# Encoder trunk of two layers: a second plain FFN set, the output projection's first half by weight chunks, and an earlier load of the first norm's scale and shift

## The chip, the cores and the metric

One core of a Trainium2 chip runs the whole kernel in one launch. Times are device microseconds (us). TensorE (PE in the profile) multiplies matrices, VectorE (DVE) and ScalarE (ACT) do elementwise work, GpSimd (POOL) small work, and SyncE (SP) issues all DMA transfers here. Each engine takes its own instructions in the order in which they stand in its queue; engines wait for each other by semaphores.

## The reference, cut to what matters

```python
x = layer_norm(x, ln_in_g, ln_in_b)                 # x: 512 tokens x 1024
for l in range(2):
    proj = x @ w_in[l]                              # 6816 columns: q, k, v of three mixers, and gates
    ...                                             # neighbourhood, differential and latent attention
    merged = sum(gates[b] * (out[b] @ w_branch[l, b]) for b in range(3))
    x = layer_norm(ALPHA * x + merged @ w_out[l], ln1_g[l], ln1_b[l])
    gu = x @ w_ffn_in[l]                            # 2 x 2816 columns
    hidden = silu(gu[..., :2816]) * gu[..., 2816:]
    x = layer_norm(ALPHA * x + hidden @ w_ffn_out[l], ln2_g[l], ln2_b[l])
```

All in float32.

## The kernel before, in words

**Products.** Each float32 operand is held as two parts, hi and lo, and a product of two matrices is three matmuls (hi by hi, hi by lo, lo by hi; `mm3`, lines L156 to L158, or `product`, L778). ACT writes hi (a copy, L138 or L221) and DVE writes lo (a difference, L139 or L222). A matmul works on 128 rows of the contraction and on up to 512 columns. The tokens are four tiles t of 128; the transposed x stands in `xth` and `xtl` as eight contraction tiles k.

**Buffers.** A weight chunk of 128 x 1024 is loaded by SP into one of two `raw` buffers, and split into one of four `whi` and one of four `wlo` buffers (`wload`, `wsplit`), or, with `wload_slots`, into slots of the pool R (38 tiles of 128 x 512), where it can stay longer. The pool H has eight tiles of 128 x 1024 (`f` in the profile; `r` is a slot of R). PSUM has four kinds of banks, two of each: `acc`, `sc`, `pv` and `tr`. A matmul that begins a new sum in a bank waits until the last sum has been read from it.

**Order.** The program is written in the order of the functions. A scheduler of the framework then places each engine's instructions, by readiness in its own model of time and by priority (`high_priority`, used in `wsplit` unless `now` is false), so an engine's queue mixes what the text has apart.

**The output projection** (`out_proj`, L701). After the merges (`merge`; L685 and L686 on DVE take the merge sums out of `acc`, ACT L224 and DVE L225 split the merged tiles into R), x times ALPHA plus the product with `w_out` is formed in two halves of 512 columns. A half's weights are four chunks of two contraction tiles. For each token tile, one `acc` bank takes 8 x 3 matmuls through all four chunks, and DVE (L711) adds it to x. Between the halves `ahead` loads the first FFN set's weights into R (`plain_weights`, four `raw` loads, each split by two ACT and two DVE instructions). After each tile of the second half, `layer_norm` (L237 statistics, L239, POOL, L252, L253) and `to_xt` (L263 transposes into `tr`, then L221 and L222 into `xth` and `xtl`) follow.

**The FFN** goes by sets of 256 gate and 256 up columns, eleven per layer. The first set is plain (`ffn_plain`): gate and up by direct products, for two halves of the tokens, in the banks `sc` and `pv`. The other ten use seven products for eight (`ffn_fast`, after Strassen), for which sums and differences of weight quarters (L839 to L841, L853) and of x's quarters (`x_sums`, four sums, each of eight R slots, from `gt` and `xs` tiles; L748 to L759 on DVE) are formed and split. In the second set, the first to use the sums, `early` is true: the products that use no sum come first, the gate's second quarter among them, and `x_sums` is called in the middle of the set. Sets go in chunks of 3, 3, 3 and 2; a chunk's product with `w_ffn_out` (`ffn_down`) stands among the next chunk's sets.

**The start.** SP issues the first x tile (L278), the tables `cons` (L282, 256 KB: the identity that the transposes use, and rotary tables), then scale and shift of the first norm (`load_gb`, L270, twice 512 KB), the second x tile, and the first weights. For tile 0, DVE's L252 needs the scale and L253 the shift; the transposes L263 need `cons` and L253's result.

Of the kernel before, what the change touches and what calls it, by code (L numbers as in the profile page):

```python
# [12 lines left out]
OP = mybir.AluOpType  # L13
# [8 lines left out]
NT = 4  # L22
KD = 8
# [58 lines left out]
def trunk(ctx, tc, x, ln_in, w_in, feat, bias, lamv, w_mla, w_mlr, w_mlv, w_branch, w_out,  # L82
# [37 lines left out]
        return dp.tile([128, 512], F32, tag="P", name="P", bufs=4)  # L120


    def wload(segs, nk, ncol):
        raw = wp.tile([128, 1024], F32, tag="raw", name="raw", bufs=2)
        rv = raw[:, :nk * ncol].rearrange("p (k c) -> p k c", k=nk)
        c = 0
        for src in segs:
            w = src.shape[1]
            nc.sync.dma_start(rv[:, :, c:c + w], src.rearrange("(k p) c -> p k c", p=128))
            c += w  # L130
        hi, lo = wsplit(raw, nk * ncol)
        return hi.rearrange("p (k c) -> p k c", k=nk), lo.rearrange("p (k c) -> p k c", k=nk)

    def wsplit(raw, n, now=True):
# [9 lines left out]
        nc.sync.dma_start(raw[:, :n], src)  # L144
        return wsplit(raw, n)

    def wload_ks(src_of, widths, steps):

        res, k = [], 0
        for n in steps:  # L150
            res.append((k, n, wload(src_of(k * 128, (k + n) * 128), n, widths)))
            k += n
        return res

# [124 lines left out]

    G.memset(expo, -0.5)  # L280
    load_x(0)
    nc.sync.dma_start(cons, cst)  # L282
    gb = load_gb(ln_in)
    na_v, na_slots = [], []
    load_x(1)
    na_v += na_value_chunks(0, (0,))
# [414 lines left out]
    def out_proj(xt, mg, l, ahead):  # L701
        act = tuple(KTiles(m) for m in mg)
        for hf in range(2):
            if hf == 1:
                ahead()
            c = slice(hf * 512, (hf + 1) * 512)
            ch = wload_ks(lambda a, e: [w_out[l, a:e, c]], 512, (2, 2, 2, 2))
            for t in range(NT):
                p = bank("acc")
                gemm_x(p, ch, slice(0, 512), act, tsl(t), KD)  # L710
                V.scalar_tensor_tensor(xt[t][:, c], xt[t][:, c], ALPHA, p, op0=OP.mult, op1=OP.add)  # L711
                if hf == 1:
                    yield t
        R.put(*mg[0], *mg[1])


# [70 lines left out]
        split(*hl, sg)  # L787
        return hl

    def plain_weights(l, m):  # L790

        chs, slots = [], []
        for base in (0, D_FF):
            c = slice(base + m * 128, base + (m + 2) * 128)
            ch, sl = wload_slots(lambda a, e: [w_ffn_in[l, a:e, c]], 256, (4, 4))
            chs.append(ch)
            slots += sl
        return chs, slots

    def ffn_plain(chs, slots):  # L800
# [12 lines left out]
    def ffn_fast(l, m, sums):  # L813


        early = not sums

        def load(t, base, kh):
            c = slice(base + m * 128, base + (m + 2) * 128)
            nc.sync.dma_start(t.rearrange("p (k c) -> p k c", k=4),  # L820
                              w_ffn_in[l, kh * 512:(kh + 1) * 512, c].rearrange("(k p) c -> p k c", p=128))
            return t

        def halved(t, now=True):
            return wsplit(t, 1024, now)

        g0, u0, u1 = load(H.get(), 0, 0), load(H.get(), D_FF, 0), load(H.get(), D_FF, 1)
        s = H.get()
        g1 = load(wp.tile([128, 1024], F32, tag="raw", name="raw", bufs=2), 0, 1)
        px, py, pz = bank("sc"), bank("pv"), bank("sc")  # L830
        product(px, halved(g0, not early), from_x(0, 0), True)
        p1 = ptile()
        A.activation(p1, px, AF.Copy)  # L833
        if early:
            product(px, halved(g1, False), from_x(1, 0), False)
            sums += x_sums()
        t1, t2, t3, t4 = sums
        with tc.high_priority():
            V.tensor_add(s, u0, u1)  # L839
            V.tensor_sub(u0, g0, u0)  # L840
            V.tensor_sub(g0, s, g0)  # L841
        product(py, halved(g0), from_sum(t2), True)
        u2 = ptile()
        V.tensor_add(u2, py, p1)  # L844
        product(pz, halved(s), from_sum(t1), True)
        product(py, halved(u0), from_sum(t3), False)
        u3 = ptile()
        V.tensor_add(u3, py, p1)
        V.tensor_add(u3, pz, u3)
        if not early:  # L850
            product(px, halved(g1), from_x(1, 0), False)
        with tc.high_priority():
            V.tensor_sub(g1, g1, g0)  # L853
        product(pz, halved(g1), from_x(1, 1), False)
        V.tensor_add(u2, pz, u2)
        product(py, halved(u1), from_sum(t4), False)
        V.tensor_add(p1, py, p1)
        H.put(s, u0, g0, u1)
        res = [hidden(px, p1)]
        res.append(hidden(u2, u3))  # L860
        return res
# [24 lines left out]
    for l in range(DEPTH):  # L886
# [21 lines left out]
        mg = [[], []]  # L908
# [57 lines left out]
            nc.sync.dma_start(xt[t], xd[t])  # L966
        gb = load_gb(ln1[l])
        plain = []
        for t in out_proj(xt, mg, l, lambda: plain.append(plain_weights(l, 0))):
            layer_norm(xt[t], *gb)  # L970
            to_xt(xt[t], t)
        H.put(*gb)
        done, sums = None, []
        for c, (m0, n) in enumerate(CHUNKS):
            sets = []
            for i in range(n):
                m = 2 * (m0 + i)
                if m0 + i == 0:
                    sets.append(ffn_plain(*plain[0]))
                else:  # L980
                    sets.append(ffn_fast(l, m, sums))
                last = m0 + i == D_FF // 256 - 1
# [107 lines left out]
```

## Time and profile before

| what | value |
|---|---|
| three timed runs | 1859.96 us median (1859.23 to 1865.12) |
| the profiled execution's own time | 1861.61 us |
| its span, first to last instruction | 1859.6 us |
| mean granted TensorE clock | 0.996 |
| PE, DVE, ACT, POOL busy | 98%, 72%, 49%, 5% of the span |
| matmuls | 11200 |

The profile lists each engine's instructions with start and duration in us from the span's start. A line of the waits says who waited for whom, how long in total, how often, and the longest. A row of a group or of the timeline names the source line, the engine, the operation, the tile written and the tiles read, and the shapes; in brackets stands how long the engine was idle before it and who ended that. Matmuls are pipelined: one begins before the record of the last one has ended. The granted clock is the share of full speed that TensorE's clock had in a stretch. The chain is the work that ended last, followed back from the end, each piece with its start and duration.

### The profile page before, as it was taken

How to read it: one execution, taken by the hardware profiler on the slowest of the kernel's cores; microseconds unless marked ns; L12 is line 12 of the kernel's file. 1: busy time of each engine (PE TensorE's matmuls, PEld its weight loads, DVE VectorE, ACT ScalarE, POOL GpSimd, SP SyncE). 2: the span in 40 equal slices, each digit the busy share in tenths (PEclk: the TensorE clock that was granted, in tenths of full speed). 3: DMA queues.
4: the chain of work that ended last, by engine and by line, in shares of the span. 5: the costliest groups of instructions: out<-in, count | busy, mean ns of one | idle time of the engine just before them, and what ended most of it. 6: DMA issues, size and time to landing. Idle time of an engine off the chain costs nothing.

```text
span 1859.6 us, 28547 instructions
## 1 busy us (share of the span) xinstructions
PE 1814.6 (98%) x11200; PEld 1617.4 (87%) x11200; DVE 1331.0 (72%) x2228; ACT 905.3 (49%) x1620; POOL 88.2 (5%) x165
## 2 busy tenths in 40 slices
PE   6999999999999899999999999999999999999997
PEld 5988899988878899999789888999888789999996
DVE  6478887665568977777756888866655698677766
ACT  3467776555433433434326677755554244343431
POOL 4100000000001000000001000000000000000001
PEclk9999999999999999999999999999999999999999
DMA  7453332223251233333445432322233512333332
GB/s 250 119 166 88 88 101 74 79 81 85 90 193 58 69 104 101 102 103 102 148 124 156 124 97 87 90 65 86 74 97 109 174 57 90 105 95 110 92 101 79
DMA packets 167765, 195.86 MB, mean 105 GB/s; under 512 B 8528, under 2 KB 132688, under 8 KB 167632
## 3 DMA queue, kind: packets, MB, share of 16 engines
q1 hardware_dynamic: 167632, 194.05, 34.5%
q8 instruction: 88, 1.44, 0.3%
q14 instruction: 45, 0.37, 0.1%
HBM read 177.24 MB, written 9.44 MB: 100 GB/s over the span
## 4 chain that ended last, share of the span: by engine, by line
PE 89%; DVE 4%; DMA 3%; ACT 2%; issue 1%; POOL 1%; POOLq 0%; SPq 0%; DVEq 0%; ACTq 0%
PE acc L156 18%; PE acc L157 18%; PE acc L158 18%; PE sc L778 11%; PE pv L778 8%; PE tr L648 2%; DVE wlo L139 1%; PE pv L491 1%; DMA raw<-in_w_ffn_in_dram 1%; ACT whi L138 1%; PE pv L656 1%; PE pv L655 1%; PE sc L477 1%; PE sc L632 1%; PE sc L631 1%
## 5 line engine op out<-in xcount | busy, mean ns | idle before, releaser
L139 DVE TENSOR_TENSOR wlo<-raw,whi 128x1024 fp32r<-128x1024 f32 (+4 forms) x242 | 288.0, 1191 | 137.0 <-ACT whi L138 132.2
L138 ACT ACTIVATE whi<-raw 128x1024 fp32r<-128x1024 f32 (+4 forms) x242 | 250.0, 1034 | 267.4 <-DMA raw<-in_w_ffn_out_dram 50.9
L138 ACT ACTIVATE whi<-f 128x1024 fp32r<-128x1024 f32 x100 | 104.9, 1057 | 222.4 <-PE acc L158 127.3
L156 PE MATMUL acc<-xth,whi 128*128 128x512 f32 x512 | 203.9, 398 | 0.1
L158 PE MATMUL acc<-xth,wlo 128*128 128x512 f32 x512 | 202.8, 396 | 0.0
L157 PE MATMUL acc<-xtl,whi 128*128 128x512 f32 x512 | 202.6, 396 | 0.0
L156 PE MATMUL acc<-whi,r 128*128 128x512 f32 (+1 forms) x504 | 194.7, 392 | 4.6 <-DVE f L711 3.9
L157 PE MATMUL acc<-wlo,r 128*128 128x512 f32 (+1 forms) x504 | 197.3, 391 | 1.1 <-DVE wlo L139 1.1
L158 PE MATMUL acc<-whi,r 128*128 128x512 f32 (+1 forms) x504 | 197.0, 391 | 0.0
L778 PE MATMUL pv<-r,whi 128*128 128x256 f32 x960 | 175.8, 282 | 9.9 <-DVE P L844 4.8
L156 PE MATMUL acc<-whi,xth 128*128 128x256 f32 (+2 forms) x544 | 161.6, 299 | 2.1 <-ACT whi L138 2.1
L157 PE MATMUL acc<-wlo,xth 128*128 128x256 f32 (+2 forms) x544 | 162.1, 299 | 1.3 <-DVE wlo L139 1.3
L158 PE MATMUL acc<-whi,xtl 128*128 128x256 f32 (+2 forms) x544 | 162.1, 299 | 0.0
L778 PEld LDWEIGHTS pv<-r,whi 128*128 128x128 f32 x960 | 148.2, 189 | 13.4 <-DVE P L844 5.2
L139 DVE TENSOR_TENSOR wlo<-f,whi 128x1024 fp32r<-128x1024 f32 x100 | 121.6, 1221 | 26.0 <-ACT whi L138 25.8
L778 PE MATMUL pv<-r,wlo 128*128 128x256 f32 x480 | 134.7, 281 | 0.0
L778 PE MATMUL sc<-xth,whi 128*128 128x256 f32 x480 | 133.9, 280 | 0.7 <-ACT P L833 0.7
L778 PE MATMUL sc<-xtl,whi 128*128 128x256 f32 x480 | 133.7, 279 | 0.0
L778 PE MATMUL sc<-xth,wlo 128*128 128x256 f32 x480 | 133.3, 279 | 0.0
L156 PEld LDWEIGHTS acc<-whi,r 128*128 128x128 f32 x504 | 94.3, 188 | 26.9 <-DVE f L711 4.7
L157 PEld LDWEIGHTS acc<-wlo,r 128*128 128x128 f32 x504 | 95.0, 188 | 22.1 <-DVE wlo L139 1.8
L158 PEld LDWEIGHTS acc<-whi,r 128*128 128x128 f32 x504 | 94.9, 188 | 21.0
(235 smaller groups left out, 4285.3 us busy)
## 6 DMA issues: line engine op xcount, KB each, us to landing
raw<-in_w_in_dram SPq DMA_DIRECT2D x64, 512.0 KB, 3.8
f<-in_w_ffn_in_dram SPq DMA_DIRECT2D x60, 512.0 KB, 3.7
raw<-in_w_ffn_out_dram SPq DMA_DIRECT2D x44, 512.0 KB, 3.8
raw<-in_w_in_dram SPq DMA_DIRECT2D x64, 256.0 KB, 3.3
raw<-in_w_ffn_in_dram SPq DMA_DIRECT2D x28, 512.0 KB, 3.6
raw<-in_w_branch_dram SPq DMA_DIRECT2D x24, 512.0 KB, 3.5
raw<-in_w_out_dram SPq DMA_DIRECT2D x16, 512.0 KB, 3.8
r<-r SPq DMA_DIRECT2D x56, 128.0 KB, 2.9
```

The lines of the kernel that those rows point to most:

```text
L138: A.activation(hi[:, :n], raw[:, :n], AF.Copy)
L139: V.tensor_sub(lo[:, :n], raw[:, :n], f32(hi[:, :n]))
L156: T.matmul(o, lh[0], rh[0], start=first, stop=False)
L157: T.matmul(o, lh[0], rh[1], start=False, stop=False)
L158: T.matmul(o, lh[1], rh[0], start=False, stop=last)
L477: T.matmul(sc, qs[j][:, tsl(t)], ks[j][1], start=False, stop=True)
L491: T.matmul(po[:, 0:256], ch_[:, tsl(k)], v, start=k == 0, stop=False)
L631: T.matmul(sc, q[0][:, tsl(t)], k[0], start=True, stop=False)
L632: T.matmul(sc, q[0][:, tsl(t)], k[1], start=False, stop=False)
L648: T.transpose(pt[:, tsl(i)], prs[i % 2][:, tsl(kp + i // 2)], ident)
L655: T.matmul(oc, v, ph[:, c], start=kt == 0, stop=False)
L778: T.matmul(o[:, c], w[a][:, j, f], x[e], start=fresh and mi == 0 and j == 0 and n == 0, stop=j == 3 and n == 2, skip_group_check=True)
```

## The change

Three things. (1) The second FFN set is computed plainly too: its weights are streamed through the `raw`, `whi` and `wlo` buffers without high priority, and `x_sums` is called once, after that set, so `ffn_fast` loses its `early` form. (2) In the first half of the output projection the loop over weight chunks is the outer one and the four token tiles are summed side by side in two `sc` and two `pv` banks; `ahead` is called within the first half, behind its loads. The second half is as before. (3) Scale and shift of the first norm are issued ahead of the tables.

```diff
@@ wload, wload_ks
-    def wload(segs, nk, ncol):
+    def wload(segs, nk, ncol, now=True):
...
-        hi, lo = wsplit(raw, nk * ncol)
+        hi, lo = wsplit(raw, nk * ncol, now)
@@ start
     load_x(0)
+    gb = load_gb(ln_in)
     nc.sync.dma_start(cons, cst)
-    gb = load_gb(ln_in)
@@ out_proj
         for hf in range(2):
-            if hf == 1:
-                ahead()
             c = slice(hf * 512, (hf + 1) * 512)
             ch = wload_ks(lambda a, e: [w_out[l, a:e, c]], 512, (2, 2, 2, 2))
+            if hf == 0:
+                ahead()
+                ps4 = [bank(i) for i in ("sc", "sc", "pv", "pv")]
+                for part in ch:
+                    for t in range(NT):
+                        gemm_x(ps4[t], [part], slice(0, 512), act, tsl(t), KD)
+                for t in range(NT):
+                    V.scalar_tensor_tensor(xt[t][:, c], xt[t][:, c], ALPHA, ps4[t], op0=OP.mult, op1=OP.add)
+                continue
             for t in range(NT):
                 p = bank("acc")
                 gemm_x(p, ch, slice(0, 512), act, tsl(t), KD)
                 V.scalar_tensor_tensor(xt[t][:, c], xt[t][:, c], ALPHA, p, op0=OP.mult, op1=OP.add)
-                if hf == 1:
-                    yield t
+                yield t
@@ plain_weights
-    def plain_weights(l, m):
+    def plain_weights(l, m, ahead):
...
-            ch, sl = wload_slots(lambda a, e: [w_ffn_in[l, a:e, c]], 256, (4, 4))
+            src = lambda a, e: [w_ffn_in[l, a:e, c]]
+            if ahead:
+                ch, sl = wload_slots(src, 256, (4, 4))
+                slots += sl
+            else:
+                ch = wload_ks(src, 256, (4, 4), False)
             chs.append(ch)
-            slots += sl
@@ ffn_fast
-        early = not sums
...
-        product(px, halved(g0, not early), from_x(0, 0), True)
+        product(px, halved(g0), from_x(0, 0), True)
...
-        if early:
-            product(px, halved(g1, False), from_x(1, 0), False)
-            sums += x_sums()
...
-        if not early:
-            product(px, halved(g1), from_x(1, 0), False)
+        product(px, halved(g1), from_x(1, 0), False)
@@ the layer's loop
                 if m0 + i == 0:
                     sets.append(ffn_plain(*plain[0]))
+                elif m0 + i == 1:
+                    sets.append(ffn_plain(*plain_weights(l, m, False)))
+                    sums = x_sums()
                 else:
                     sets.append(ffn_fast(l, m, sums))
```

What it moves in the queues, at the places that the prediction speaks of. First PE, at the end of layer 0's merges (a space: the row stands in both; +: only in the changed program). The `acc` rows are merges, the `sc` and `pv` rows the projection's first half, which read the merged tiles `r`.

```order
 L157 MATMUL acc<-r_85,whi 128x512
 L158 MATMUL acc<-r_84,wlo 128x512
+L157 MATMUL sc<-wlo,r_94 128x512
+L158 MATMUL sc<-whi,r_95 128x512
+L156 MATMUL pv<-whi,r_94 128x512
+L157 MATMUL pv<-wlo,r_94 128x512
+L158 MATMUL pv<-whi,r_95 128x512
+L158 MATMUL pv<-whi,r_87 128x512
+L156 MATMUL pv<-whi,r_94 128x512
 L156 MATMUL acc<-r_108,whi 128x512
```

These are seven of the 26 first-half matmuls that now stand between merges, and so ahead of the last merge's end; 24 + 46 follow it. Next DVE, a little later: the sums of the first half in the old program, between the splits of the first FFN set's weights (`r<-raw`).

```order
 L222 TENSOR_TENSOR r_111<-raw,r_110 128x512
 L222 TENSOR_TENSOR r_93<-raw,r_92 128x512
-L711 SCALAR_TENSOR_TENSOR f_115<-f_115,acc 128x512
-L711 SCALAR_TENSOR_TENSOR f_117<-f_117,acc 128x512
-L237 BN_STATS ring<-f_115 128x6
-L237 BN_STATS ring<-f_117 128x6
 L222 TENSOR_TENSOR r_107<-raw,r_106 128x512
 L222 TENSOR_TENSOR r_109<-raw,r_108 128x512
```

The first-half sums (L711, now L713) stood behind three of the four splits and are now behind all four, among the splits of the second half's weights (`wlo<-raw`):

```order
+L139 TENSOR_TENSOR wlo<-raw,whi 128x1024
+L713 SCALAR_TENSOR_TENSOR f_115<-f_115,sc 128x512
+L139 TENSOR_TENSOR wlo<-raw,whi 128x1024
+L237 BN_STATS ring<-f_115 128x6
+L713 SCALAR_TENSOR_TENSOR f_117<-f_117,sc 128x512
+L713 SCALAR_TENSOR_TENSOR f_118<-f_118,pv 128x512
+L237 BN_STATS ring<-f_117 128x6
+L713 SCALAR_TENSOR_TENSOR f_116<-f_116,pv 128x512
 L237 BN_STATS ring<-f_118 128x6
-L139 TENSOR_TENSOR wlo<-raw,whi 128x1024 x2
-L711 SCALAR_TENSOR_TENSOR f_116<-f_116,acc 128x512
+L139 TENSOR_TENSOR wlo<-raw,whi 128x1024
```

Six rows of L713 and L237 now stand between the second half's second and third `wlo`. Last DVE again, where the norm of the last two token tiles meets the second set's weights.

```order
 L253 SCALAR_TENSOR_TENSOR f_118<-f_118,ring,f_114 128x512
 L222 TENSOR_TENSOR xtl<-tr,xth 128x4x128
 L253 SCALAR_TENSOR_TENSOR f_118<-f_118,ring,f_114 128x512
+L139 TENSOR_TENSOR wlo<-raw,whi 128x1024
 L237 BN_STATS ring<-f_116 128x6
+L139 TENSOR_TENSOR wlo<-raw,whi 128x1024
+L222 TENSOR_TENSOR xtl<-tr,xth 128x4x128 x2
```

Two splits of the second plain set's weights stand ahead of the next copies of `xtl`, and so of the last tile's norm.

More of the change, by code (lines that the diff above doesn't have):

```diff
@@ L145, in wload_flat, with wload_ks @@
         return wsplit(raw, n)
-    def wload_ks(src_of, widths, steps):
+    def wload_ks(src_of, widths, steps, now=True):
         res, k = [], 0
         for n in steps:
-            res.append((k, n, wload(src_of(k * 128, (k + n) * 128), n, widths)))
+            res.append((k, n, wload(src_of(k * 128, (k + n) * 128), n, widths, now)))
             k += n
@@ L822, in load, with halved @@
             return t
-        def halved(t, now=True):
-            return wsplit(t, 1024, now)
+        def halved(t):
+            return wsplit(t, 1024)
         g0, u0, u1 = load(H.get(), 0, 0), load(H.get(), D_FF, 0), load(H.get(), D_FF, 1)
@@ L968, in trunk @@
         plain = []
-        for t in out_proj(xt, mg, l, lambda: plain.append(plain_weights(l, 0))):
+        for t in out_proj(xt, mg, l, lambda: plain.append(plain_weights(l, 0, True))):
             layer_norm(xt[t], *gb)
@@ L972, in trunk @@
         H.put(*gb)
-        done, sums = None, []
+        done = None
         for c, (m0, n) in enumerate(CHUNKS):
```

## The prediction

> **What bounds the kernel now.** I read the page first: busy time, and the chain that ended last.
>
> ```profile
> span 1859.6 us, 28547 instructions
> PE 1814.6 (98%) x11200; PEld 1617.4 (87%) x11200; DVE 1331.0 (72%) x2228; ACT 905.3 (49%) x1620; POOL 88.2 (5%) x165
> PE 89%; DVE 4%; DMA 3%; ACT 2%; issue 1%; POOL 1%; POOLq 0%; SPq 0%; DVEq 0%; ACTq 0%
> ```
>
> TensorE is busy for all but 45.0 us. So a change can gain only where PE waits, where its clock is down, or by fewer matmuls; this one adds matmuls. The stretches (us, PE busy, PEld, DVE, ACT, POOL, granted clock, DMA share, GB/s) show where PE waits near the edits: layer 0's output projection, then layer 0's second FFN set, then the same two places of layer 1.
>
> ```profile
> 535.00:540.00 5.00, 4.27 (x19) 3.08 (x17) 1.72 (x3) 2.25 (x4) 0.00 (x0) 1.00 1.07 349
> 540.00:545.00 5.00, 3.48 (x9) 2.76 (x10) 4.45 (x8) 1.21 (x3) 0.00 (x0) 0.70 0.39 127
> 545.00:550.00 5.00, 5.00 (x22) 4.01 (x22) 1.00 (x2) 0.00 (x0) 0.00 (x0) 0.96 0.33 105
> ...
> 605.00:610.00 5.00, 4.78 (x43) 4.58 (x41) 5.00 (x9) 3.29 (x6) 0.00 (x0) 1.00 0.00 0
> ...
> 615.00:620.00 5.00, 2.57 (x20) 2.16 (x18) 5.00 (x8) 3.27 (x4) 0.00 (x0) 1.00 0.34 105
> 620.00:625.00 5.00, 3.09 (x24) 2.89 (x24) 4.97 (x6) 0.12 (x1) 0.00 (x0) 1.00 0.02 3
> 625.00:630.00 5.00, 4.58 (x38) 4.58 (x39) 3.53 (x6) 2.49 (x3) 0.00 (x0) 1.00 0.00 0
> ```
> ```profile
> 1455.00:1460.00 5.00, 3.39 (x16) 2.40 (x15) 3.22 (x6) 2.10 (x4) 0.00 (x0) 1.00 0.85 268
> ...
> 1525.00:1530.00 5.00, 4.50 (x38) 4.31 (x37) 4.39 (x7) 2.39 (x5) 0.00 (x0) 1.00 0.36 110
> 1530.00:1535.00 5.00, 3.52 (x28) 3.11 (x26) 4.92 (x7) 3.02 (x6) 0.00 (x0) 1.00 0.37 105
> 1535.00:1540.00 5.00, 2.76 (x18) 2.76 (x19) 4.97 (x6) 0.82 (x1) 0.00 (x0) 0.87 0.01 2
> 1540.00:1545.00 5.00, 4.22 (x30) 3.92 (x30) 3.23 (x4) 1.54 (x2) 0.00 (x0) 0.79 0.00 0
> ```
>
> PE misses 2.25 us in the projection of layer 0 and 1.61 in layer 1; at the second set it misses 4.98 (605 to 630) and 4.98 (1525 to 1545). There DVE is full: PE waits for it. The clock column counts too: 0.70 and 0.96 of 5 us are 1.7 us of lost cycles after layer 0's projection wait, 0.87 and 0.79 another 1.7 us in layer 1's second set.
>
> **The change part by part.** The price of a matmul is its interval in a run without a wait, from the chain (start, us, what) and from two successive starts:
>
> ```profile
> 628.51 5.65 PE sc L778 x48
> ```
> ```profile
> 577.18 0.39 PE L157 MATMUL acc<-wlo,r 128*128 128x512 f32 x1
> 577.41 0.39 PE L158 MATMUL acc<-whi,r 128*128 128x512 f32 x1
> ```
>
> So 0.118 us for 256 columns, 0.23 for 512. A record lasts 0.16 us longer than its interval, so each wait costs 0.16 more than the idle time shown.
>
> *More matmuls.* A set by seven products is 7 x 2 x 4 x 3 = 168 matmuls of 256 columns, a plain one 2 x 2 x 2 x 8 x 3 = 192. The 24 more cost half of that 5.65 us row: 2.83 per layer, **+5.65** in all, on PE, with nothing to hide them.
>
> *The second set's waits.* They are waits for DVE, which makes the sums of x while PE already needs them. After the change the sums are made under a plain set that reads none of them, 192 x 0.118 = 22.6 us. The first and the last row of that DVE work:
>
> ```profile
> 592.20 0.68 DVE L748 TENSOR_TENSOR gt<-xth 128x512 f32<-128x512 f32 x1
> ...
> 618.82 0.68 DVE L222 TENSOR_TENSOR r<-gt,r 128x512 fp32r<-128x512 f32 x1
> ```
>
> It took 27.3 us, with splits for the set itself in between, which no longer press. All waits go: 4.98 + 4.98, four waits per layer at 0.16 (1.3), and the clock's 1.7: **-13.0**. What is late next there is nothing I can find: the third set's first buffer for weights comes free when the plain set's gate half ends, 48 matmuls (5.65) before it starts, and a split needs 2.3.
>
> *The projection.* Who ended its waits:
>
> ```profile
> PE acc L156 <- DVE f L711: 2.2, 1, 2.2
> ```
>
> The sums L711 that free the two banks stand in DVE's queue behind splits that wait for weights. With four banks in the first half and acc in the second, that wait goes, in both layers: 2.25 + 1.61 + 0.3 + 1.7 of clock = **-5.9**. But the loads themselves don't get faster, and I ask who is late next. The rows, all of layer 0 but the last two:
>
> ```profile
> 522.43 1.07 ACT whi L138
> 523.52 1.24 DVE wlo L139
> 524.78 4.69 DMA raw<-in_w_ffn_in_dram
> ...
> 533.21 5.67 DMA raw<-in_w_ffn_in_dram
> ...
> 1442.62 4.77 DMA raw<-in_w_ffn_in_dram
> ...
> 1451.13 4.96 DMA raw<-in_w_ffn_in_dram
> ```
> ```profile
> 528.10 0.69 DVE L685 SCALAR_TENSOR_TENSOR f<-f,acc 128x512 f32<-128x512 f32 x1
> 535.91 1.29 DVE L222 TENSOR_TENSOR r<-raw,r 128x512 fp32r<-128x512 f32 x2 [2.13 <-ACT r L221]
> ```
> ```profile
> 535.25 1.15 ACT L221 ACTIVATE r<-raw 128x512 fp32r<-128x512 f32 x2 [2.54 <-DMA raw<-in_w_ffn_in_dram]
> 556.66 1.06 ACT L138 ACTIVATE whi<-raw 128x1024 fp32r<-128x1024 f32 x1 [3.78 <-DMA raw<-in_w_out_dram]
> ```
>
> The last merge ends at 528.0 now. In the changed order 26 first-half matmuls stand ahead of its end, so it ends at 528.0 + 26 x 0.232 = 534.1 (no PE time is lost by that). The fourth weight chunk of the first half takes that merge's whi buffer, and on both ACT and DVE the splits of all four plain loads stand behind it. So the chain starts at 534.1: split 2.3, and the raw buffer is free at 536.4. From there two plain loads and then the second half's second chunk pass through this buffer. A leg is a load plus 1.95 us (from the start of ACT's two halves at 535.25 to the end of DVE's at 537.20). With 3.8 and 4.9 us for the loads (between the 3.78 waited here and 5.67) they end at 542.2 and 549.0; the chunk's load of 3.9 at 552.9, its whi at 554.0, its wlo at 555.2. PE, without a wait, has 46 + 24 matmuls of the first half after the merge (16.2 us: 550.3) and 7 of the second (552.0): it waits 2.0 for whi and 0.3 for wlo. Then it has 14 matmuls (3.2 us), and the third chunk's wlo is 3.7 + 1.2 us away, since six L713 and L237 (0.61 each, a little under half of that 1.29) stand ahead of it: 1.6 more. That is 3.9 in layer 0. In layer 1 the second of the plain loads above took 4.96 against 5.67; with legs 0.4 shorter it is 2.6. So **+6.5**: the wait moves from between the halves into the second half. No row shows these waits; their ends are 0 and, with 5.67 for each load, about 9 per layer. I take 3.9 and 2.6, nearest to the loads of those very tiles.
>
> *The second plain set's splits.* Its four streamed chunks stand on DVE; two of them (1.2 each) now between layer_norm's L253 of tile 2 and the xtl copy of tile 1. PE's second four transposes of tile 2 need the bank that this copy frees:
>
> ```profile
> 582.04 0.67 DVE L222 TENSOR_TENSOR xtl<-tr,xth 128x512 fp32r<-128x512 f32 x1
> ```
> ```profile
> 584.28 0.60 PE L263 MATMUL tr<-cons,f 128*128 128x128 f32 x4
> ```
>
> Today the bank is free 1.6 us before PE comes to them. It comes 2.4 later: I take 0.75 per layer, **+1.5**, ends 0 and 2.4 per layer. The waits for tile 1's and 2's norm just ahead of it stay.
>
> *The start.* Norm's scale and shift are issued 0.47 us sooner:
>
> ```profile
> 1.16 0.42 SPq L282 DMA_DIRECT2D cons<-in_cst_dram  x1
> 1.63 0.90 SPq L270 DMA_DIRECT2D f<-in_ln_in_dram  x2
> ```
> ```profile
> 8.45 1.61 DVE L252 SCALAR_TENSOR_TENSOR f<-f,ring,f 128x512 f32<-128x512 f32 x2 [2.63 <-DMA f<-in_ln_in_dram]
> ```
> ```profile
> 11.25 1.97 PE L263 MATMUL tr<-cons,f 128*128 128x128 f32 x8 [11.25 <-DVE f L253]
> ```
> ```profile
> DMA to landing us min/median/max: 3.9/3.9/3.9
> ```
>
> DVE, and through it PE, waits for them. The tables, issued at 2.1, may take their 3.9 us or twice that and still land before 10.7, when PE needs them. **-0.5**, ends 0 and -0.9 (the bytes of the tables ahead of them too).
>
> The sum: 5.65 - 13.0 - 5.9 + 6.5 + 1.5 - 0.5 = **-5.75**. It is made on the profiled execution, 1861.61 us with a span of 1859.6. The median of the three runs, 1859.96, is 1.65 less, about one fall of the clock; I subtract from the median and get **1854.2**.
>
> Here the clock's fall is a term, 3.4 of the 18.9 us removed. The trace shows it at half for 3.4 us after idle time of 2.25. The Trainium skill (TensorE: Matmul & The Clock Gate, Part 1) says that the clock goes back to half after at least one idle window of about 3.4 us, and advises against gaps over about 3 us. By that rule neither fall would be there; the trace disagrees, and I keep the 3.4 us.
>
> **Rivals.** A measurement of this kernel can tell about 0.3% (5.6 us) from no change.
>
> *Weights in time (0.20).* The second half doesn't wait: -5.75 - 6.5 = -12.25, 1847.7. For it: both its ends of the price are open, and two loads took 3.8. Against: the queue order of DVE alone leaves 1.6 per layer once PE waits at all.
>
> *The clock's falls aren't mine to win (0.13).* The two longest waits of the second set are the same in both layers; in layer 0 they brought no fall, in layer 1 they did; so a fall hangs on where a wait lies in time, and the timed runs may not have them, nor give them back: -5.75 + 3.4, 1857.6. By the Trainium skill's rule above there is nothing to win back either.
>
> ```profile
> PE pv L778 <- DVE P L844: 2.4, 1, 2.4
> PE pv L778 <- DVE r L222: 1.3, 1, 1.3
> ```
>
> *Slower: the second half starves (0.08).* If each load of the chain takes the 5.67 us seen at 533.21, the second chunk's wlo comes at 536.4 + 2 x 7.62 + 5.67 + 2.3 = 559.6 against 552.2 on PE: 7.4 + 1.6, and two falls of 1.7: 12.4 per layer instead of 3.9 and 2.6. That is -5.75 + 18.3: 1872.5. It decides from about 1 us more per load than I take. Against: loads of 3.8.
>
> *The change doesn't take the second set's waits away (0.07):* DVE, still full, makes the third set wait instead, all but the clock's 1.7: -5.75 + 11.3, 1865.5. Against: DVE gets 22.6 us more before the sums are needed.
>
> *The four banks (0.02).* Each first-half step goes round four accumulators. If that kept the clock down for its 96 matmuls, they'd cost 22.3 us more per layer, 1898.8. The Trainium skill names such a fault (same page, A second HAM failure mode: psum-queue depth-cycling). In the trace PE goes from pv to sc and back at 625 to 630 with the clock at 1.00.
>
> **How the numbers follow.** The forecast has 0.50, with its own range 1851 to 1857; it lies at the edge of what can be told, so I split it: 0.30 faster, 0.20 same. Faster: 0.30 + 0.20 = 0.50. Same: 0.20 + 0.13 + part of the third-set case (0.07) = 0.40. Slower: 0.10, the starved second half and the four banks. The range 1847 to 1860 takes in the first two rivals and leaves out the rest.
>
> **What would show it.** Right: no idle PE between the halves, nothing for DVE sums in the second set, clock at 1.00 there; new PE waits for whi L138 and wlo L139 in the second half of out_proj, some 3.9 and 2.6 us; 11200 + 48 = 11248 matmuls; the first transposes near 10.75. Wrong: a second half without waits (then 1847.7), PE waiting for DVE in the third set, or waits there long enough to bring the clock down.

## The result and the profile after

The changed kernel takes 1847.76 us (median of 6 runs, 1845.85 to 1850.09), the kernel before 1860.35 (6 runs): a ratio of 0.9928, 95% interval 0.9916 to 0.9941, so 12.6 us less. Forecast were 1854.2 and 5.75 less: the direction held, the size did not. The profiled execution took 1850.09 us with a span of 1847.0; its span, too, is 12.6 us under that of before.

The page of the changed kernel, its first lines:

```profile
span 1847.0 us, 28601 instructions
PE 1814.9 (98%) x11248; PEld 1617.9 (88%) x11248; DVE 1309.9 (71%) x2204; ACT 897.8 (49%) x1612; POOL 90.1 (5%) x165
PE 89%; DVE 5%; DMA 3%; ACT 1%; issue 1%; SPq 0%; POOLq 0%; DVEq 0%; POOL 0%; ACTq 0%
```

There are 48 more matmuls, as announced, and PE is idle for 32.1 us instead of 45.0. The stretches (columns as before) of the projection's second half and of the second set, layer 0, then the same two places of layer 1:

```profile
545.00:550.00 5.00, 5.00 (x23) 4.00 (x23) 2.64 (x3) 2.12 (x2) 0.00 (x0) 1.00 0.57 181
550.00:555.00 5.00, 4.08 (x18) 2.96 (x16) 5.00 (x8) 1.93 (x2) 0.00 (x0) 1.00 0.39 136
...
605.00:610.00 5.00, 5.00 (x46) 5.00 (x45) 3.96 (x7) 1.64 (x3) 0.00 (x0) 1.00 0.00 0
...
615.00:620.00 5.00, 5.00 (x47) 5.00 (x46) 2.45 (x2) 1.72 (x3) 0.00 (x0) 1.00 0.00 0
```
```profile
1465.00:1470.00 5.00, 4.67 (x20) 3.48 (x19) 3.08 (x4) 1.06 (x1) 0.00 (x0) 1.00 0.42 121
...
1525.00:1530.00 5.00, 5.00 (x47) 5.00 (x46) 1.93 (x3) 1.66 (x2) 0.00 (x0) 1.00 0.00 0
```

The second set has no idle PE and the clock is 1.00. What is left in the second half of the projection is 0.92 and 0.33 us (1.08 and 0.49 with the 0.16 of each wait by the prediction's reckoning; by the matmuls' starts 1.25 and 0.49). One more number stands in these rows: 46 to 47 matmuls. A row counts every matmul that touches its 5 us, and a record lasts 0.28 us; at the prediction's price of 0.118 that makes 5.28 / 0.118 = 45. So the matmuls come faster than that. The longest of PE's waits, in total:

```profile
PE tr L263 <- DVE f L253: 9.1, 1, 9.1
PE acc L157 <- DVE wlo L139: 3.5, 5, 1.1
PE tr L263 <- DVE xtl L222: 3.0, 4, 1.1
PE acc L156 <- ACT whi L138: 2.2, 2, 1.6
PE pv L784 <- DVE P L853: 2.0, 5, 0.5
```

The waits for the sums L711 and for the sums of x (DVE P L844, r L222) are gone. The first row is the start: 9.1 us, where 11.25 stood.

Both traces number the same matmuls (24 are added per layer, at a known place), so the difference of their start times tells where the time went. "Forecast" is the prediction's own terms, split by place:

| stretch | before | after | difference | forecast |
|---|---|---|---|---|
| start and mixers, to matmul 2600 | 448.28 | 445.68 | -2.60 | -0.5 |
| rest of layer 0's mixers, projection | 125.92 | 123.36 | -2.56 | -0.2 |
| first set with the norm's tail, layer 0 | 26.58 | 27.35 | +0.77 | +0.75 |
| second set, layer 0 | 25.68 | 21.80 | -3.88 | -2.8 |
| third set, layer 0 | 19.88 | 19.62 | -0.26 | 0 |
| to the end of layer 1's projection | 838.80 | 837.74 | -1.06 | +0.8 |
| first set, layer 1 | 26.58 | 27.37 | +0.79 | +0.75 |
| second set, layer 1 | 26.96 | 21.78 | -5.18 | -4.5 |
| third set, layer 1 | 19.88 | 19.61 | -0.27 | 0 |
| the rest | 281.85 | 283.53 | +1.68 | 0 |

The rows leave out 4.73 us per layer, from the norm's first transposes to the first set's first matmul, and 9.7 us behind the last matmul; both are the same in the two traces.

Against the forecast, three terms gained more than was said: the projections by 2.4 + 1.9, the start by 2.1, the second sets by 1.1 + 0.7. But a row compares one execution with one other. The last row was +0.3 when the same kernel was profiled again (run e5, below), so its 1.68 belongs to this one execution. The profiles of the experiments below that leave the part in question as it was, and all tiles in their places, give the same stretches again:

| stretch | in profiles with the old part | with the new part |
|---|---|---|
| to matmul 2600 | 447.50 to 448.28 (3) | 444.97 to 445.89 (5) |
| layer 0's projection row | 123.34 to 125.92 (4) | 122.40 to 123.40 (5) |
| to the end of layer 1's projection | 836.31 to 838.80 (4) | 837.05 to 841.16 (5) |
| second set, both layers | 25.67 to 26.96 (4) | 21.77 to 21.81 (6) |

The start and the second set stand clear of that scatter. The projection's gain doesn't: 125.92, with a fall of the clock in it, was the longest of the four, and on the means about 1.2 us are won in layer 0 and none in layer 1.

### The profile page after: what moved, and what is told of

It reads as the page before. It is cut to its first block, busy times and chain, and to the rows that moved or that the text cites. A ratio compares the mean times of both kernels' runs of the same rounds, so it can differ in the third digit from the quotient of the medians.

```text
span 1847.0 us, 28601 instructions
## 1 busy us (share of the span) xinstructions
PE 1814.9 (98%) x11248; PEld 1617.9 (88%) x11248; DVE 1309.9 (71%) x2204; ACT 897.8 (49%) x1612; POOL 90.1 (5%) x165
## 4 chain that ended last, share of the span: by engine, by line
PE 89%; DVE 5%; DMA 3%; ACT 1%; issue 1%; SPq 0%; POOLq 0%; DVEq 0%; POOL 0%; ACTq 0%
PE acc L157 18%; PE acc L158 18%; PE acc L156 17%; PE sc L784 9%; PE pv L784 7%; DVE wlo L139 2%; PE tr L648 2%; PE sc L156 1%; DMA f<-in_w_ffn_in_dram 1%; PE sc L158 1%; PE sc L157 1%; PE pv L157 1%; PE pv L158 1%; PE pv L156 1%; PE pv L491 1%
## 5 line engine op out<-in xcount | busy, mean ns | idle before, releaser
L138 ACT ACTIVATE whi<-raw 128x1024 fp32r<-128x1024 f32 (+3 forms) x246 | 254.3, 1034 | 289.4 <-PE acc L157 54.1
L139 DVE TENSOR_TENSOR wlo<-raw,whi 128x1024 fp32r<-128x1024 f32 (+3 forms) x246 | 293.6, 1195 | 132.2 <-ACT whi L138 129.0
L157 PE MATMUL acc<-wlo,r 128*128 128x512 f32 (+1 forms) x440 | 171.3, 390 | 2.2 <-DVE wlo L139 2.2
L158 PE MATMUL acc<-whi,r 128*128 128x512 f32 (+1 forms) x440 | 170.7, 389 | 0.0
L156 PE MATMUL acc<-whi,r 128*128 128x512 f32 (+1 forms) x440 | 169.0, 390 | 0.6 <-ACT whi L138 0.5
L784 PE MATMUL pv<-r,whi 128*128 128x256 f32 x864 | 156.0, 280 | 2.3 <-DVE P L853 2.0
L784 PEld LDWEIGHTS pv<-r,whi 128*128 128x128 f32 x864 | 132.3, 188 | 5.2 <-issue 2.8
L784 PE MATMUL pv<-r,wlo 128*128 128x256 f32 x432 | 120.5, 279 | 0.0
L156 PEld LDWEIGHTS acc<-xth,whi 128*128 128x128 f32 x512 | 96.3, 188 | 19.5 <-ACT f L672 0.7
L157 PEld LDWEIGHTS acc<-xtl,whi 128*128 128x128 f32 x512 | 96.4, 188 | 18.8
L158 PEld LDWEIGHTS acc<-xth,wlo 128*128 128x128 f32 x512 | 96.4, 188 | 18.7
```

The lines of the kernel that those rows point to most:

```text
L138: A.activation(hi[:, :n], raw[:, :n], AF.Copy)
L139: V.tensor_sub(lo[:, :n], raw[:, :n], f32(hi[:, :n]))
L156: T.matmul(o, lh[0], rh[0], start=first, stop=False)
L157: T.matmul(o, lh[0], rh[1], start=False, stop=False)
L158: T.matmul(o, lh[1], rh[0], start=False, stop=last)
L784: T.matmul(o[:, c], w[a][:, j, f], x[e], start=fresh and mi == 0 and j == 0 and n == 0, stop=j == 3 and n == 2, skip_group_check=True)
```

## The experiments

**The whole again, and each part alone.** The measure for all that follows is the changed kernel itself.

> The changed kernel once more, unchanged, as the measure for the runs beside it: 12.6 us under before, in every theory.

Measured: 1847.71 us, ratio 0.9935 (0.9922 to 0.9948). Its waits in the second half were 0.62 in layer 0 and 1.13 in layer 1: the sum, 1.75, is that of the first profile (1.74); its split between the layers is not a constant.

The start alone is the kernel before with two lines exchanged:

```diff
+    gb = load_gb(ln_in)
     nc.sync.dma_start(cons, cst)
-    gb = load_gb(ln_in)
```

> The kernel before with one part of the change: norm's scale and shift are loaded ahead of the tables. Theory A (the forecast's term: only the 0.47 us of the earlier issue counts): the first transposes start near 10.75, the median is 0.5 us under before, 1859.8. Theory B (the bytes count too: scale and shift no longer wait behind the 256 KB of the tables, and the first projections keep that gain): the first transposes start near 9.1 as in the changed kernel, the median is 2.6 under before, 1857.8, and PE's waits at the projection and in the second FFN set stay as before.

Measured: 1857.50 us against 1859.48, ratio 0.9993 (0.9984 to 1.0003), which cannot tell 0.5 from 2.6. The trace can: the first transposes come at 9.17, as in theory B,

```profile
9.17 2.14 PE L263 MATMUL tr<-cons,f 128*128 128x128 f32 x8 [9.17 <-DVE f L253]
```

and matmul 2600 starts at 445.72, 2.56 us before that of the kernel before. So the gain comes from the start alone. On the means of the table above it is 2.3.

The second set alone is the changed kernel with `out_proj` and the order of loads of before.

> The kernel before with the second FFN set plain and the sums of x behind it, nothing else. Theory B (the forecast's terms hold here: +5.65 for 48 matmuls, -13.0 for the waits, +1.5 for the splits ahead of the copy): 5.85 under before, 1854.5. Rival C (what the forecast missed, 6.9 us, lies in this part: its matmuls cost less or its waits cost more than taken): 12.7 under before, 1847.7. 11248 matmuls in both; no PE wait for the sums of x.

Measured: 1851.31 us against 1859.48, ratio 0.9964 (0.9951 to 0.9976), that is 8.2 by the medians, 4.5 to 9.1 by the interval. That leaves out C and leaves B in. The second set took 21.81 us in layer 0, as in the changed kernel; B had 22.65.

The projection alone is the kernel before with the new `out_proj`.

> The kernel before with the output projection's first half contraction outside, nothing else. Theory A (the forecast's terms: -5.9 for the wait between the halves, +6.5 for new waits in the second half): 0.6 over before, 1860.9, with PE waits of 3.9 and 2.6 in the second half. Theory B (the second chunk of the second half comes in time, only the third chunk's low half is late, 1.25 and 0.49 as in the changed kernel): 5.9 - 1.7 = 4.2 under before, 1856.1.

Measured: 1856.70 us against 1859.48, ratio 0.9994 (0.9985 to 1.0003). The waits are those of theory B. Those of layer 0, then of layer 1, each the only one in its stretch:

```profile
PE acc L157 <- DVE wlo L139: 1.1, 1, 1.1
```
```profile
PE acc L157 <- DVE wlo L139: 0.2, 1, 0.2
```

The time is not B's 4.2: 2.8 by the medians, and by the interval anything from 2.8 less to 0.6 more, so a gain of the projection by itself isn't shown. In its profile the clock still fell twice, at 578 and 619 us (in that of before at 542 and 1539), and the mean granted clock of its 11 timed runs is that of the kernel before, 0.9974. So the 1.7 us of clock that the forecast booked to layer 0's projection were not won by this part alone. With the second set alone it was 0.9984. The three parts add up to 2.0 + 8.2 + 2.8 = 13.0 by the medians and to some 9 by the ratios, against 12.3 and 12.1 for the whole in e5's comparison: the same within the intervals, with the second set as the main part.

**The start: issue or bytes.** One column of the tables instead of all of them ahead of scale and shift:

```diff
-    nc.sync.dma_start(cons, cst)
+    nc.sync.dma_start(cons[:, 0:1], cst[:, 0:1])
     gb = load_gb(ln_in)
+    nc.sync.dma_start(cons[:, 1:512], cst[:, 1:512])
```

> The kernel before, with one column of the tables (512 bytes) loaded where the whole tables were loaded, norm's scale and shift behind it as before, and the rest of the tables behind those. The loads of scale and shift are issued as late as in the kernel before, but without the 256 KB ahead of them. Theory A (the forecast: only the issue 0.47 us earlier counts): no gain, first transposes at 11.2. Theory B (the bytes ahead count): first transposes at 9.4 to 9.8.

Measured: ratio 1.0003 (0.9992 to 1.0015), and in the trace a place between the theories. Its loads, DVE and PE, then DVE of the changed kernel:

```profile
1.64 0.90 SPq L270 DMA_DIRECT2D f<-in_ln_in_dram  x2
```
```profile
7.52 1.61 DVE L252 SCALAR_TENSOR_TENSOR f<-f,ring,f 128x512 f32<-128x512 f32 x2 [1.77 <-DMA f<-in_ln_in_dram]
```
```profile
10.32 1.97 PE L263 MATMUL tr<-cons,f 128*128 128x128 f32 x8 [10.32 <-DVE f L253]
```
```profile
6.97 1.15 DVE L252 SCALAR_TENSOR_TENSOR f<-f,ring,f 128x512 f32<-128x512 f32 x2 [0.92 <-DMA f<-in_ln_in_dram]
```

L252 starts at 8.45 before, 7.52 with the bytes gone, 6.97 with the earlier issue as well. So by these rows the bytes are 0.93 and the issue 0.55 of the 1.48 us there; two more profiles with the old start (e2, e3) have L252 at 8.55 and 8.09, so the parts are sure to about 0.4. Matmul 2600 starts at 446.07 in this trace, against 447.50 to 448.28 with the old start and 444.97 to 445.89 with the new one: there, too, the bytes are the larger part. The timed runs do not show it, so it rests on one trace.

The tables one step later still (in the changed kernel, behind the second tile of x):

> The changed kernel with the tables loaded one step later still, behind x's second tile. If the bytes ahead count for x's second tile too (theory B), DVE starts that tile's statistics earlier, and up to 0.5 us more is won; if the transposes then wait for the tables, the first of them start later than 9.1 and up to 1 us is lost. Within 1 us of the changed kernel either way.

Measured: ratio 0.9955 (0.9942 to 0.9968), some 4 us more than the changed kernel, so the expectation was wrong. PE now waits for the tables:

```profile
PE tr L263 <- DMA cons<-in_cst_dram: 10.3, 1, 10.3
...
PE tr L263 <- POOL f L249: 2.6, 1, 2.6
```

The tables, issued at 2.57, land at 10.2, and the other wait that is new, 2.6 us for GpSimd, ends at 30.6. In the changed kernel, issued at 2.10, they landed at 8.8 and were there when DVE was done at 9.1. The forecast gave them up to twice 3.9 us; they take 6.7 there and 7.6 here.

**The second half's wait: which buffer.** The forecast began its chain of loads at the last merge's end, because the fourth weight chunk was to take that merge's buffer. In the changed kernel's trace, ACT, the splits of that chunk and of the second half's third, and PE, the last matmuls of the first chunk and of the last merge:

```profile
528.50 1.06 ACT L138 ACTIVATE whi<-raw 128x1024 fp32r<-128x1024 f32 x1 [2.83 <-PE pv L158]
...
551.34 1.06 ACT L138 ACTIVATE whi<-raw 128x1024 fp32r<-128x1024 f32 x1 [2.19 <-DMA raw<-in_w_out_dram]
```
```profile
528.02 0.39 PE L158 MATMUL pv<-whi,r 128*128 128x512 f32 x1
...
531.28 0.39 PE L158 MATMUL acc<-r,wlo 128*128 128x512 f32 x1
```

The split started when the first chunk was used up, 3 us before the merge's end; it is the same in layer 1 (1440.50 against 1443.68). The merge's end itself was forecast well: 534.1, less the 2.6 of the start, against 531.67. And from there the loads went by the way that was forecast. SP's plain loads, DVE's split of the last of them, and ACT's split of the second half's second chunk:

```profile
530.85 2.81 SPq L206 DMA_DIRECT2D raw<-in_w_ffn_in_dram  x2
...
536.41 0.37 SPq L206 DMA_DIRECT2D raw<-in_w_ffn_in_dram  x1
```
```profile
543.09 1.29 DVE L222 TENSOR_TENSOR r<-raw,r 128x512 fp32r<-128x512 f32 x2 [4.34 <-ACT r L221]
```
```profile
548.09 1.06 ACT L138 ACTIVATE whi<-raw 128x1024 fp32r<-128x1024 f32 x1 [1.82 <-PE pv L158]
```

The fourth chunk's `raw` buffer takes the plain loads issued at 530.85 and 536.41 and then, free at 544.38, the second chunk. The legs are 5.5 and 8.0 us (forecast 5.75 and 6.85); from the first split's start to the second chunk's low half, ready at 550.41, it is 21.9 us (forecast 21.1). PE, whose second half begins at 547.85, needs that low half at about 550.4. Begun at 531.67, the same chain would have been some 3 us late, by this estimate.

To give the forecast its premise, the first chunk's buffer was held until the merge's result was there:

```diff
+                G.tensor_tensor(hold, f32(ch[0][2][0][:, 0, 0:1]), f32(mg[0][7][:, 0:1]), op=OP.add)
```

> The changed kernel, with one 1-element operation on GpSimd that reads the first half's first weight chunk and the last merge's result, so that the buffer of that chunk comes free only after the last merge; the fourth chunk must then take the merge's buffer, as the forecast assumed. Theory B (the forecast's chain of loads was right, but its start was too late by the 3 us between the first chunk's last use and the merge's end): the fourth chunk's split starts 3 to 5 us later, the whole chain of loads moves with it, and PE waits 3.5 to 4.5 us instead of 1.25 in the second half of layer 0 and about 2 to 3 instead of 0.49 in layer 1: 4 to 6 us over the changed kernel, 1852 to 1854, more by 1.7 for each fall of the clock. Rival D (the second half's loads don't hang on that buffer): within 1 us of the changed kernel, 1847.8.

Measured: 1855.76 us, ratio 0.9979 (0.9969 to 0.9988), some 8 us more than the changed kernel, but its PE waits in the second halves were 0.41 and 0.62 only. The time is beyond even theory B's 4 to 6 us, and its waits did not come. The 512-column matmuls of the first 500 us had become slower, 0.233 us instead of 0.230 on the mean. The new operation wrote a tile of 4 bytes of its own, which lay ahead of the weight buffers and moved them. So the same once more with its result in a free column of `ring`, which moves no other tile:

> The changed kernel with the holding operation of the earlier run, its result now in a free column of the ring of statistics instead of a tile of its own, so that no tile lies at another address than in the changed kernel. Theory D (what cost 6 to 8 us in the earlier run was the pace of the matmuls, 0.233 us instead of 0.230 in the first 500 us, that came with the shifted addresses; the later split of the fourth chunk costs next to nothing because the loads take the buffers as they come free): within 1 us of the changed kernel, pace 0.230, PE waits of about 0.4 and 0.6 in the second half. Theory B (the held buffer itself costs): 4 to 6 us over the changed kernel.

Measured: 1847.70 us, ratio 0.9933 (0.9921 to 0.9945): theory D, no difference in time. ACT's and SP's rows show why:

```profile
532.64 1.04 ACT L138 ACTIVATE whi<-raw 128x1024 fp32r<-128x1024 f32 x1
...
539.04 1.15 ACT L221 ACTIVATE r<-raw 128x512 fp32r<-128x512 f32 x2 [0.74 <-DMA raw<-in_w_ffn_in_dram]
542.64 1.15 ACT L221 ACTIVATE r<-raw 128x512 fp32r<-128x512 f32 x2 [2.44 <-DMA raw<-in_w_ffn_in_dram]
```
```profile
533.05 2.71 SPq L206 DMA_DIRECT2D raw<-in_w_ffn_in_dram  x2
...
538.61 0.37 SPq L206 DMA_DIRECT2D raw<-in_w_ffn_in_dram  x1
...
541.03 9.94 SPq L129 DMA_DIRECT2D raw<-in_w_out_dram  x4
```

The fourth chunk is split at 532.64, 4.1 us later than in the changed kernel and 1.1 later than the forecast had it (534.1, less the 2.6 of the start). But its `raw` buffer then passes one of the plain loads, not two: the second plain load (533.05) and the fourth (538.61) went through the other buffer, which had come free first. So the loads went by another way than in the changed kernel, and most of the delay is gone by the second half: by the matmuls' starts PE waits 0.65 us there in layer 0 and 1.49 in layer 1, 2.1 in all against 1.7. The run shows what holding the buffer costs; the forecast's whole chain, with a late start and the old way of the loads, it does not show.

**The wait that is left.** In the changed kernel, DVE's queue from the second chunk's low half on:

```profile
549.18 1.23 DVE L139 TENSOR_TENSOR wlo<-raw,whi 128x1024 fp32r<-128x1024 f32 x1 [1.06 <-ACT whi L138]
550.33 0.69 DVE L237 BATCH_NORM_STATS2 ring<-f 128x6 f32<-128x512 f32 x1
550.93 0.67 DVE L713 SCALAR_TENSOR_TENSOR f<-f,sc 128x512 f32<-128x512 f32 x1
...
553.31 0.69 DVE L237 BATCH_NORM_STATS2 ring<-f 128x6 f32<-128x512 f32 x1
553.91 1.21 DVE L139 TENSOR_TENSOR wlo<-raw,whi 128x1024 fp32r<-128x1024 f32 x1
```

ACT has the third chunk's high half at 552.40 (551.34 + 1.06); its low half starts at 553.91, behind the six L713 and L237. That is the forecast's "1.6 more", here 1.5. To put those sums behind that split, their factor was read from a column worked out from the third chunk:

```diff
-                for t in range(NT):
-                    V.scalar_tensor_tensor(xt[t][:, c], xt[t][:, c], ALPHA, ps4[t], op0=OP.mult, op1=OP.add)
...
+            G.tensor_scalar(alpha, f32(ch[2][2][0][:, 0, 0:1]), 0.0, ALPHA, op0=OP.mult, op1=OP.add)
+            for t in range(NT):
+                V.scalar_tensor_tensor(xt[t][:, c0], xt[t][:, c0], alpha, ps4[t], op0=OP.mult, op1=OP.add)
```

> The changed kernel with the first half's four sums made dependent on the second half's third weight chunk, so that on DVE they stand behind that chunk's split instead of ahead of it (addresses unmoved). Theory B (the wait that is left, 1.25 and 0.49, is the third chunk's low half queued behind those sums and the halves of the norm's statistics): both waits go, 1.7 us under the changed kernel. Rival F (that chunk's load is what is late): the waits stay, or the sums come too late for the norm and PE waits as much at the transposes: no change or slower.

Measured: 1849.21 us, ratio 0.9940 (0.9928 to 0.9952): no gain is seen, but the interval is too wide to leave out 1.7 us. The trace decides. DVE, and what PE waited for in layer 0's second half:

```profile
552.87 1.23 DVE L139 TENSOR_TENSOR wlo<-raw,whi 128x1024 fp32r<-128x1024 f32 x1 [1.93 <-ACT whi L138]
554.18 1.41 DVE L717 SCALAR_TENSOR_TENSOR f<-f,ring,sc 128x512 f32<-128x512 f32 x2
555.51 1.40 DVE L717 SCALAR_TENSOR_TENSOR f<-f,ring,pv 128x512 f32<-128x512 f32 x2
556.83 1.22 DVE L139 TENSOR_TENSOR wlo<-raw,whi 128x1024 fp32r<-128x1024 f32 x1
```
```profile
PE acc L157 <- DVE wlo L139: 0.4, 1, 0.4
PE acc L156 <- DVE f L721: 0.4, 1, 0.4
```

The third chunk is on time, as theory B has it, and the fourth now stands behind the sums, and the second half's own sums (L721 here) behind the statistics. By the matmuls' starts PE waits 1.34 us in layer 0 and 0.53 in layer 1, 1.9 in all against 1.7. So the wait moves and doesn't go: the outcome of rival F, though not for its first reason, a late load. In both orders PE waits about as long for DVE.

**The pace of the matmuls.** A tile that nothing reads, of 4, 64 or 96 bytes, ahead of the weight buffers (a tile is taken to fill whole steps of 32 bytes, so 4 count as 32; no trace shows an address):

```diff
+    pad = cp.tile([128, 1], F32, name="pad")
...
+    G.memset(pad, 0.0)
```

> The changed kernel with one more tile of 4 bytes that nothing reads, placed ahead of the weight buffers: they and all that lies behind them move by 32 bytes. Theory D (addresses set the pace): 512-column matmuls of the first 500 us at 0.233 us instead of 0.230, about 6 us over the changed kernel, waits as in it. Rival E (the pace of the earlier run came from its GpSimd operation, its order or the chip's moment): same as the changed kernel within 1 us.

> The changed kernel with a tile of 64 bytes that nothing reads ahead of the weight buffers, which move by 64 bytes instead of 32. Theory G (the pace hangs on whether the weights lie on a multiple of 64 bytes): as the changed kernel, 512-column matmuls of the first 500 us at 0.230 us. Theory H (the changed kernel's own place, an odd multiple of 64, is itself a bad one for those matmuls that run at 0.2334): faster than the changed kernel by up to 4 us. Theory I (any move costs): slower by 6 to 10 us as with 32 bytes.

> The changed kernel with a tile of 96 bytes that nothing reads ahead of the weight buffers. In the changed kernel they lie 64 bytes off a multiple of 128, where all that they are multiplied with begins; with 32 bytes more it is 96, with 64 more 0, with 96 more 32. So far: 64 off gave 0.2315 us for 512 columns and 0.1170 for 256, 96 off 0.2330 and 0.1175, 0 off 0.2285 and 0.1196. Theory J (only the distance to the multiple of 128 counts, 32 off being like 96 off): pace and time as with 32 bytes, 8 to 10 us over the changed kernel. Rival K (each place has a pace of its own, or it is another buffer behind them whose place counts): anything from 4 us under to 10 us over the changed kernel.

The runs were compared with the kernel before in three groups, so the ratios stand side by side; "off" is the distance of the weight buffers from a multiple of 128 bytes, where `xth`, `xtl` and R begin, worked out from the kernel's list of tiles. The paces are means over all matmuls of a size, without the waits.

| kernel | off | us | ratio | 512 columns | 256 columns |
|---|---|---|---|---|---|
| changed (e5) | 64 | 1847.71 | 0.9935 (0.9922 to 0.9948) | 0.2315 | 0.1169 |
| 32 more (e7) | 96 | 1857.52 | 0.9988 (0.9980 to 0.9997) | 0.2330 | 0.1175 |
| 64 more (e9) | 0 | 1851.85 | 0.9952 (0.9941 to 0.9964) | 0.2285 | 0.1196 |
| 96 more (e12) | 32 | 1859.65 | 0.9992 (0.9983 to 1.0001) | 0.2330 | 0.1181 |

With 4184 matmuls of 512 columns and 5752 of 256, the paces alone make +9.7, +3.0 and +13.2 us against e5 for the three versions; the ratios make +9.9, +3.2 and +10.6.

Theory D holds: the tile alone costs about what e4 cost. Of G, H and I none: with 64 bytes more, 512 columns go faster and 256 slower. J holds: 32 off is like 96 off. The chain (start, us, what), late in layer 0, for the changed kernel, then 96, 0 and 32 off:

```profile
876.05 2.83 PE pv L784 x24
```
```profile
878.93 2.80 PE pv L786 x24
```
```profile
878.32 2.88 PE pv L786 x24
```
```profile
880.48 2.84 PE pv L786 x24
```

24 matmuls of 256 columns at 0.1179, 0.1167, 0.1200 and 0.1183 us. The same pace, by rows of PE's timeline and of the chain, in the changed kernel's second set and in its third up to a wait:

```profile
607.74 0.28 PE L157 MATMUL pv<-xtl,whi 128*128 128x256 f32 x1
...
608.64 0.28 PE L156 MATMUL pv<-xth,whi 128*128 128x256 f32 x1
```
```profile
625.81 2.72 PE pv L784 x24
628.53 3.85 PE sc L784 x34
```

Eight intervals in 0.90 us, then 24 in 2.72: 0.1133. A wait of 0.3 us, over at 636.81, ends it, and the matmuls behind it go at 0.1179, as the row of 876.05 shows. The same change comes at the same matmul in the profiles of e2, e5 and e11. The second set as a whole: 192 in 21.80 us, 0.1135 each; with the buffers 96, 0 and 32 off it took 22.43, 23.04 and 22.73 us. The first plain set, whose weights lie in R and so 0 off, goes at 0.120 in all of them. The second set reads only `xth` and `xtl`, which don't move, and the weight buffers, which do. But all tiles behind the weight buffers move with them, so whether the weights' own place counts, or that of the others, isn't separated. No version tried here is clearly faster than the changed kernel.

## Why the prediction was wrong in size

- *More matmuls, +5.65:* the count held, the price did not. 0.118 was the pace of the old second set, behind its waits; the plain set goes at 0.1135. With 192 x 0.1135 against 168 x 0.118 the term is +1.97 per layer, **+3.9**, and the third set gained 0.5 by going on at that pace.
- *The second set's waits, -13.0:* all gone in both layers, nothing late in the third set. The second sets together went from 52.64 to 43.58, -9.06, against -7.35 forecast; the price of the matmuls is the difference. (The idle time in the forecast's rows is 4.98 and 5.00 us, not twice 4.98.) Of the clock's falls, the one in the second set was won: each of the four profiles with the old set has one there, in one of its two layers, and none of the ten with the new set has one. The one in layer 0's projection stood in the profile of before alone. Over the timed runs of e5's comparison the mean granted clock is 0.9973 before and 0.9980 after, worth 1.3 us where the forecast had 3.4 in all.
- *The projection, -5.9:* the waits for the sums L711 are gone, as said, but the price was that of one execution. By the matmuls' starts they were 2.41 and 1.77 us in the profile of before, with a fall of the clock, and 1.39 and 0.74 in e1, 1.85 and 1.29 in e2, 1.57 and 1.89 in e10, without one: on the mean 3.2 us where the forecast took 4.2, and a fall of 1.7 in one of four.
- *The second half's new waits, +6.5:* **this is the step that failed.** Its 1.6 us for the third chunk behind six L713 and L237 was right in kind, and one link of it, 1.5, in size (PE waited 1.25 and 0.49; 0.62 and 1.13 in e5). Its other part, the second chunk late by 2.0 + 0.3 in layer 0 and less in layer 1, did not happen at all, because "the fourth weight chunk of the first half takes that merge's whi buffer" was false: the chunk took the buffer of the first chunk, and the chain began at 528.50 and not at the merge's end, 531.67. The links behind it, two plain loads through the same `raw` buffer and then the second chunk, were right. In place of 6.5 stands **1.7**. That the late start would have cost the wait rests on the rows; e6, which made it late, changed the way of the loads as well.
- *The second plain set's splits, +1.5:* measured +0.77 and +0.79. PE's waits for that copy are four, 3.0 us together, where they were two, 2.1.
- *The start, -0.5:* measured **-2.6**, on the means -2.3. The bounds had the earlier issue and, at the end of the range, the bytes; 0.55 and 0.93 were both there at L252. The rest came behind it: the two halves of L252 took 1.15 instead of 1.61 us, and a wait of 0.7 us for GpSimd went, as e1 shows by keeping all of 2.56 to matmul 2600. It is the second half of L252 that took 0.48 instead of 0.95 us. In the kernel before, GpSimd's L248 ran beside it (8.51 to 9.79); in the changed kernel L248 starts at 8.93, when L252 is over. The two go together in the other profiles looked at as well (e1, e2, e5, e10), but no run separates them.
- *Rivals:* "weights in time" gave 1847.7, and that is the time, but only in part for its reason: of the waits it spoke of 4.8 us stayed away and 1.7 came, and the start and the pace made up the rest. "The clock's falls aren't mine to win" is right for layer 0's projection and wrong for the second set. The starved second half, the third set's wait and the four banks are refuted (PE's clock is 1.00 in the projection).

## What to carry to other kernels

When a chain of loads is to be forecast, look first which buffer its head takes: here it was one that came free 3 us before the one reckoned with, and the wait of the forecast hung on that. A probe that delays the head can send the later loads another way, and then tells less than it seems to. Before a wait is booked as a gain, see in a second profile whether it is as long there. Take the price of an added matmul from rows whose operands lie as the new ones will, and look for a second pace of the same shape in the trace before trusting the first. A probe that brings its own tile can move everything behind it: here 4 bytes cost 10 us, so let a probe write into something that exists.

## What the runs showed of the hardware

The pace of matmuls hangs on where tiles lie in memory. 256 columns took 0.1133, 0.1167, 0.1179 or 0.1200 us, 512 columns on average 0.2285 to 0.2330, by the distance of the weights from a multiple of 128 bytes, and at one and the same place 0.1133 up to a wait of 0.3 us and 0.1179 behind it. What in the chip does this no run here shows. The Trainium skill (TensorE: Matmul & The Clock Gate, section Back-to-back issue gap) gives N / 2.4 + 2.5 ns for isolated matmuls, by which 256 and 512 columns would take 0.109 and 0.216 us, and for a stream with weight loads about 131 ns at 512 columns. All the paces here lie above these figures, and on the place of the operands that section says nothing.

The clock fell to half without an idle window as long as the fall. The stretches around two of the three falls in e1's profile:

```profile
575.00:580.00 5.00, 4.22 (x23) 4.22 (x24) 5.00 (x10) 0.96 (x2) 0.79 (x2) 0.66 0.00 0
615.00:620.00 5.00, 2.59 (x14) 2.39 (x13) 4.97 (x7) 1.06 (x1) 0.00 (x0) 0.72 0.01 3
```

The first follows waits of 0.85 and 1.21 us among the transposes; the changed kernel has the same two waits there and no fall, so the waits alone don't decide it. The second begins within a wait of 2.4 us. Each fall lasted 3.41 us. The Trainium skill (same page, Part 1) gives at least one idle window of about 3.4 us as the condition. From its first matmul to its last, no profile here has one (the longest idle time is 2.61 us, in e11), and yet nine of the fourteen have one to three falls, after waits in the transposes, the projection, the old second set or the start of layer 1.
